# One decoder layer on one core: small rearrangements from the first projection to the MLP, and a merge whose weights are spread by matmuls alone

## The chip, the cores and the metric

The kernel runs on one core of one Trainium2 chip. The metric is the device time of one launch in microseconds (us), the median of several runs. Matmuls run on PE (TensorE), elementwise work on DVE (VectorE), ACT (ScalarE) and POOL (GpSimd), and SP (SyncE) issues the DMAs. Engines work side by side and meet at semaphores; each runs its own instructions in a fixed order.

## The reference, cut to what matters

A prompt group (2048 tokens) and a sample group (8 requests of 8 tokens with 2048 cached positions) pass through one layer, in float32:

```python
proj = rms_norm(x, ln1_g) @ w_in
q, k = head_rms(q, q_norm_g), head_rms(k, k_norm_g)        # 8 heads x 64
att = dilated_attention(q, k, v, ...)                      # 3 branches (128,1) (512,4) (2048,16),
                                                           # merged by their softmax denominators
r, k, v, xw, xa, xg = token_shifted(proj[..., 3 * A_W:])   # RWKV-7 columns
w_log = -softplus(-(w0 + tanh(xw) @ w_lora2)) - 0.5
a = sigmoid(a0 + xa @ a_lora2)
kk = kk / max(sqrt(sum(kk * kk, -1)), 1e-12)               # per head
y, S = wkv_scan(...)                                       # state update per token
bonus = sum(r * k * r_k, -1) * v                           # per head
mixed = concat([att, rw])
h = x + mixed @ w_out
y = h + square(relu(rms_norm(h, ln2_g) @ w_mlp1)) @ w_mlp2
```

The merge is `num / den` with `num = sum over branches of exp(mx - mall) * o`: each branch's output (64 dims per head) is multiplied by one weight per token and head.

## The kernel before, in words

The program is written as Python generators and handed to a scheduler that simulates the engines, fixes the order of each engine's instructions and adds the waits. Pieces marked urgent (the recurrence) go ahead of filler (the projection). Most products of two float32 operands are done as three matmuls of a rounded high part and a low remainder: `h` and `l` at the end of a name (`wh`/`wl`, `mh`/`ml`).

Times in the profiled execution:

1. **0 to about 1220 us, first stage.** The input projection (L332 for the recurrence's columns, L792 for q, k, v) is the filler. Between its matmuls runs the RWKV recurrence, in 9 units (8 of the prompt, 1 of the sample) of 4 head pairs `p`. `prep` of each unit and pair issues, among others: the two low-rank products (L394 with rows 0 to 63 of the tile `th`, L396 with rows 64 to 127), the sum of squares per head (L424, `sel2` as a 32-column stationary operand at column position `32 * p`), eight pairs of 64x64 products into `ps` (L433, L434), and the bonus sum (L438, a full 128x128 operand `blk1`).
2. **About 1220 to 1607 us, dilated attention** of four head pairs p = 0 to 3: scores (L1074, L1075), masks and maxima on DVE, exponentials on ACT, transposes (L1092), outputs (L1099). Tiles `pts` (4 buffers) take the transposed weights from PSUM. The merge of pair p (p = 0 to 2) runs as a side strand within the attention of pair p + 1; that of p = 3 has nothing beside it. A merge computes the normalised weights `scw` (3 branches x 128 per partition), splits them into a high and a low part `wh`, writes these to DRAM (`wD`, L1177) and reads them back as `wrow` (L1180) with 512 tokens in a row, and spreads them over the 64 dims of a head by 12 matmuls of 512 columns (L1187, stationary operand `wsel`); DVE multiplies each result into `ob` and adds the branches.
3. **1607 to 1904 us, output projection** (L1441) in 6 columns of 352 tokens, with the sample's attention between its matmuls: its cached keys and values come in 40 + 40 DMAs of 512 KB (`kv`, L1245 and L1278). Behind each column `square_sums` (L1409) forms the sums of squares that the second norm needs.
4. **1904 to 3359 us, MLP** in three token groups `g` of 2 x 352 tokens and eight rounds `r` each, by a Strassen-like scheme of seven products: `normed` (L1497 on PE, L1506 on DVE, `sums_b` L1476 to L1479 on POOL) prepares a group's operand, L1546 is the first product, L1592 the second. Weight tiles `wr` come by DMA (L1533, L1584), 8 buffers for the first. `reload` (L1486) fetches the next group's `h` (2.8 MB) back from DRAM.

All DMAs that the change touches are issued by SP, in one order.

Of the kernel before, what the change touches and what calls it, by code (L numbers as in the profile page):

```python
# [17 lines left out]
P = 128  # L18
# [19 lines left out]
def host_inputs(inp):  # L38
# [39 lines left out]
    out["sel2"] = f((ii[:, None] // 64) == np.arange(32)[None, :])  # L78
# [7 lines left out]
    sl = np.zeros((P, 4, P), np.float32)  # L86
    for ty in range(2):
        for g in range(4):
            for part in range(2):
                sl[part * 8 + g * 2 + ty, g, ty * 64:(ty + 1) * 64] = 1  # L90
# [10 lines left out]
    out["kc"] = f(keys(kc).reshape(8, 1280, 4, P).transpose(0, 2, 3, 1))  # L101
    out["vc"] = f(keys(vc).reshape(8, 10, P, 512))
# [69 lines left out]
def _build(ctx, tc, nc, I, O, dbg, upto):  # L172
# [73 lines left out]
    G.memset(tw, 0.0)  # L246

# [104 lines left out]
    def lora_prep(load):  # L352

        th = rw.tile([P, UT], F32, name="th")
        load(th)
        act(th[0:64], th[0:64], AF.Tanh)
        return th
# [29 lines left out]
    def prep(st, p, n, r, k, v, sample):  # L387
        nch = n // C
        L1, BK, GC, qS, qd, b1, vsc = (st[x] for x in ("L1", "BK", "GC", "qS", "qd", "b1", "vsc"))
        th = st["lora"]  # L390
# [3 lines left out]
        PE.matmul(zw[:, :n], lwa[0:64, ps_], th[0:64, :n], start=True, stop=True)  # L394
        za = ms()
        PE.matmul(za[:, :n], lwa[64:128, ps_], th[64:128, :n], start=True, stop=True)  # L396
# [63 lines left out]
    def bias_vectors():  # L460
# [17 lines left out]
        for h in range(8):  # L478
            nc.sync.dma_start(out=bvD[h:h + 1].rearrange("h p b n -> h p (b n)"), in_=bc(bv1[h:h + 1].rearrange("h b n -> h (b n)"), 1, P))
            yield  # L480
# [232 lines left out]
    def unit(g):  # L713
# [13 lines left out]
        st["lora"] = lora_prep(lambda t: nc.sync.dma_start(out=t, in_=xsD[12, :, us]))  # L727
# [22 lines left out]
    def sample_unit():  # L750
        st = new_unit()

        def padded(js, t):
            n = len(range(*js.indices(15)))
            c = rw3.tile([P, 3, NS], F32, name="xsc", bufs=1)[:, :n]
# [6 lines left out]
        st["lora"] = lora_prep(lambda t: padded(slice(12, 13), t.unsqueeze(1)))  # L762
# [351 lines left out]
    def merge(p, ob, st):  # L1114
# [60 lines left out]
        wD = dat.tile([6, 4, 8, P], F32, name="wD")  # L1175
        for g in range(4):
# [29 lines left out]
    wrow = at.tile([P, 3, 512], F32R, name="wrow")  # L1206
    G.memset(wrow.bitcast(F32), 0.0)
# [20 lines left out]
    def sample_attention(b, psa):  # L1228
# [12 lines left out]
        for k0, n, parts in runs:  # L1241
            ps = psa.tile([P, 512], F32, name="sc", tag="sp", bufs=2)
            for k1 in range(0, n, 256):
                kt = kv_tile().rearrange("p (q n) -> p q n", q=4)
                nc.sync.dma_start(out=kt, in_=I["kc"][b, :, :, k0 + k1:k0 + k1 + 256].rearrange("p q n -> q p n"))  # L1245
# [23 lines left out]
        for q0 in range(0, 11, 4):  # L1269
            bl = blocks[q0:q0 + 4]  # L1270
            vts = []
            for y in range(0, len(bl), 2):
                vt = kv_tile().rearrange("p (q n) -> p q n", q=2)
                kb = bl[y][2]
                if kb is None:
                    nc.sync.dma_start(out=vt[:8, 0], in_=vSD[b * 8:b * 8 + 8])
                else:
                    nc.sync.dma_start(out=vt, in_=I["vc"][b, kb:kb + 2].rearrange("k q f -> q k f"))  # L1278
# [137 lines left out]
    with pool(name="wo2", bufs=1) as wo2, pool(name="pwo", bufs=4, space=PSUM, side="right") as pwo, pool(name="psa", bufs=1, space=PSUM) as psa, pool(name="pst", bufs=1, space=PSUM) as pst:  # L1416
# [5 lines left out]
        for c0 in range(0, NT, NC_):  # L1422
# [9 lines left out]
            for k in order:  # L1432
                if (k, c0) not in mixed:
                    mixed[k, c0] = mix_panel(we if k >= 4 else wo2, k, c0)
            for o in range(KT):
                ps = pwo.tile([P, 512], F32, name="pwo")
                i = 0
                for k in order:
                    mh, ml = mixed[k, c0]
                    for a, b in ((woh, mh), (woh, ml), (wol, mh)):  # L1440
                        PE.matmul(ps[:, :NC_], a[k][:, o * P:(o + 1) * P], b, start=(i == 0), stop=(i == 3 * KT - 1))  # L1441
                        i += 1
# [5 lines left out]
            for i in range(NC_ // SQ):  # L1448
                square_sums(h, c0 // SQ + i, i * SQ, pst.tile([P, 512], F32, name="pst"), wo2)
# [7 lines left out]
    with pool(name="mm", bufs=1, side="right") as mm, pool(name="pm", bufs=8, space=PSUM) as pm:  # L1457
# [31 lines left out]
        def normed(g, h, mb):  # L1489
# [112 lines left out]
        for g in range(3):  # L1602
            late = []
            nh = reload(1) if g == 0 else None
            for r in range(8):
                hs = []
                for f in (2 * r, 2 * r + 1):
# [3 lines left out]
                    if g == 1 and r == 0:  # L1611
                        nh = nh or reload(2)
# [7 lines left out]
                second(r, hs, h, last, g * 2 * HT, beside)  # L1620
                for _ in beside:
# [38 lines left out]
```

## Time and profile before

| what | value |
|---|---|
| median of 3 timed runs | 3361.71 us (3357.81 to 3361.98) |
| profiled execution, own time | 3364.24 us |
| its span in the trace | 3362.5 us |
| PE busy | 3156.2 us, 94% |
| DVE, ACT, POOL busy | 2156.4, 1472.5, 982.1 us |
| DMA engines, mean | 124 GB/s over the span |

The profiled execution lies 1.74 us above its span and 2.53 us above the median of the timed runs. In the profile a busy PE is a pipelined one: the duration of a matmul is longer than the distance to the next, so costs of single matmuls are read as the distance from start to start. "PEclk" is the granted clock as a share of 2.4 GHz; the lower level, 1.2 GHz, reads 0.5.

### The profile page before, as it was taken

How to read it: one execution, taken by the hardware profiler on the slowest of the kernel's cores; microseconds unless marked ns; L12 is line 12 of the kernel's file. 1: busy time of each engine (PE TensorE's matmuls, PEld its weight loads, DVE VectorE, ACT ScalarE, POOL GpSimd, SP SyncE). 2: the span in 40 equal slices, each digit the busy share in tenths (PEclk: the TensorE clock that was granted, in tenths of full speed). 3: DMA queues.
4: the chain of work that ended last, by engine and by line, in shares of the span. 5: the costliest groups of instructions: out<-in, count | busy, mean ns of one | idle time of the engine just before them, and what ended most of it. 6: DMA issues, size and time to landing. Idle time of an engine off the chain costs nothing. (4 is left out here: it accounts for less than half of the span.)

```text
span 3362.5 us, 63750 instructions
## 1 busy us (share of the span) xinstructions
PE 3156.2 (94%) x24214; PEld 2847.8 (85%) x24214; DVE 2156.4 (64%) x4539; ACT 1472.5 (44%) x3497; POOL 982.1 (29%) x1146
## 2 busy tenths in 40 slices
PE   5999989999998979999899689999999999999999
PEld 5866876787787868888688579999899999899999
DVE  4655676677566435566544487676976767967675
ACT  4454665555545447677222233232432323433332
POOL 1003442354043100111000154343543434533332
PEclk9998999999998989999899789999999999999999
DMA  5465466456457393333767423222232222222222
GB/s 167 134 183 154 116 183 168 119 134 189 128 128 196 89 284 130 109 92 89 235 220 241 151 63 85 66 81 67 90 120 63 88 64 82 91 66 85 64 88 73
DMA packets 369495, 418.45 MB, mean 124 GB/s; under 512 B 117251, under 2 KB 230718, under 8 KB 369188
## 3 DMA queue, kind: packets, MB, share of 16 engines
q1 hardware_dynamic: 369188, 414.38, 41.5%
q8 instruction: 190, 3.11, 0.4%
q14 instruction: 117, 0.96, 0.1%
HBM read 325.52 MB, written 93.46 MB: 125 GB/s over the span
## 5 line engine op out<-in xcount | busy, mean ns | idle before, releaser
L185 ACT ACTIVATE wh<-wr 128x512 fp32r<-128x512 f32 x744 | 463.3, 625 | 812.5 <-PE pm L1592 473.7
L1592 PE MATMUL pm<-fh,wl 128*128 128x352 f32 x1536 | 495.7, 323 | 8.8 <-DVE wl L1466 8.8
L1592 PE MATMUL pm<-fh,wh 128*128 128x352 f32 x1536 | 493.4, 324 | 0.0
L1592 PE MATMUL pm<-fl,wh 128*128 128x352 f32 x1536 | 492.1, 323 | 0.3 <-DVE fl L182 0.3
L1546 PE MATMUL pm<-ml,wh 128*128 128x352 f32 x1344 | 436.6, 325 | 12.3 <-DVE ml L182 12.3
L1546 PE MATMUL pm<-mh,wh 128*128 128x352 f32 x1344 | 437.0, 326 | 11.3 <-ACT wh L185 8.4
L1546 PE MATMUL pm<-mh,wl 128*128 128x352 f32 x1344 | 434.1, 324 | 8.2 <-DVE wl L1466 8.1
L182 DVE TENSOR_TENSOR res<-pm,res 128x352 f32<-128x352 f32 x384 | 198.4, 522 | 287.8 <-PE pm L1592 285.0
L1466 DVE TENSOR_TENSOR wl<-wr,wh 128x512 fp32r<-128x512 f32 x432 | 362.0, 838 | 3.1 <-ACT wh L185 0.6
L1592 PEld LDWEIGHTS pm<-fh,wl 128*128 128x128 f32 x1536 | 289.9, 189 | 9.8 <-DVE wl L1466 9.8
L1592 PEld LDWEIGHTS pm<-fl,wh 128*128 128x128 f32 x1536 | 289.1, 189 | 0.8 <-DVE fl L182 0.6
L1592 PEld LDWEIGHTS pm<-fh,wh 128*128 128x128 f32 x1536 | 289.0, 189 | 0.6 <-ACT mh L185 0.2
L1546 PEld LDWEIGHTS pm<-ml,wh 128*128 128x128 f32 x1344 | 255.1, 190 | 18.3 <-DVE ml L182 18.0
L1546 PEld LDWEIGHTS pm<-mh,wh 128*128 128x128 f32 x1344 | 255.0, 190 | 13.5 <-ACT wh L185 10.1
L1546 PEld LDWEIGHTS pm<-mh,wl 128*128 128x128 f32 x1344 | 254.8, 190 | 11.2 <-DVE wl L1466 11.1
L182 DVE TENSOR_TENSOR wl<-wr,wh 128x512 fp32r<-128x512 f32 (+1 forms) x216 | 149.1, 692 | 156.8 <-ACT wh L185 149.5
L792 PE MATMUL pj<-wh,nh 128*128 128x256 f32 (+1 forms) x816 | 239.5, 294 | 6.3 <-ACT qks L185 5.0
L792 PE MATMUL pj<-wh,nl 128*128 128x256 f32 (+1 forms) x816 | 237.7, 292 | 4.6 <-DVE nl L182 4.6
L332 PE MATMUL pj<-nh,wh 128*128 128x512 f32 (+3 forms) x600 | 222.3, 374 | 16.3 <-ACT nh L185 9.9
L792 PE MATMUL pj<-wl,nh 128*128 128x256 f32 (+1 forms) x816 | 235.3, 289 | 0.0
L332 PE MATMUL pj<-nl,wh 128*128 128x512 f32 (+3 forms) x600 | 223.3, 373 | 4.6 <-DVE nl L182 4.5
L332 PE MATMUL pj<-nh,wl 128*128 128x512 f32 (+3 forms) x600 | 218.8, 366 | 0.3 <-DVE wl L182 0.3
(305 smaller groups left out, 7120.0 us busy)
## 6 DMA issues: line engine op xcount, KB each, us to landing
wr<-in_w SPq DMA_DIRECT2D x384, 256.0 KB
wr<-in_wr SPq DMA_DIRECT2D x120, 256.0 KB
wr<-in_wq SPq DMA_DIRECT2D x96, 256.0 KB
kv<-in_kc SPq DMA_DIRECT2D x40, 512.0 KB
kv<-in_vc SPq DMA_DIRECT2D x40, 512.0 KB
xsD<-xst SPq DMA_DIRECT2D x56, 256.0 KB
xrkv<-xsD SPq DMA_DIRECT2D x32, 384.0 KB
vt<-vD SPq DMA_DIRECT2D x48, 256.0 KB
```

The lines of the kernel that those rows point to most:

```text
L182: V.tensor_tensor(out, a, b, op)
L185: S.activation(out, in_, func, bias=bias, scale=scale, **kw)
L332: PE.matmul(ps[:m, :n], a[:, k, :m], b[h * 4 + k][:, c0:c0 + n], start=(h == 0 and i == 0), stop=(h == 1 and i == 11))
L792: PE.matmul(out, a[h * 2 + k][:, i * P:i * P + m], b[:, k, :], start=(h == 0 and q == 0 and i % 2 == 0), stop=(h == 3 and q == 5 and (i % ...
L1466: (G if pooled else V).tensor_tensor(wl, w, wh.bitcast(F32), ALU.subtract)
L1546: PE.matmul(ps, a[:, k], b[:, k], start=(n == 0), stop=(n == 11))
L1592: PE.matmul(ps, a[:, f], b[:, cs], start=(i == 0), stop=(i == 11))
```

## The change

First stage: `th` becomes two zero-padded halves, so that L394 and L396 contract over all 128 partitions; `sel2` becomes a slice of a wider table, so that L424 writes all 128 columns; L438 moves ahead of the `ps` products; the prompt's low-rank input comes in two DMAs of 64 partitions and the sample's through a tile and two POOL copies.

Attention: the merge reads `wh` directly as the moving operand. For each of the 12 results there are now 4 blocks of 128 columns times high and low part, 96 matmuls per pair instead of 12, and no `wD`, `wrow`. `wsel` is four times as large and comes in four DMAs through four `pts` buffers.

Sample attention: `kc` and `vc` lie in memory so that each partition's 4 KB are one piece. Output projection: in the first column, groups of four outputs take the recurrence's panels first.

MLP: `square_sums` of the last column moves behind round 0 of the first group; `reload` moves from round 0 to round 1; in group 0 `sums_b` runs on DVE for two of four blocks.

```diff
-    out["sel2"] = f((ii[:, None] // 64) == np.arange(32)[None, :])
+    out["sel2"] = f((ii[:, None] // 64) == np.arange(-96, 128)[None, :])
...
-    out["kc"] = f(keys(kc).reshape(8, 1280, 4, P).transpose(0, 2, 3, 1))
-    out["vc"] = f(keys(vc).reshape(8, 10, P, 512))
+    out["kc"] = f(keys(kc).reshape(8, 5, 256, 4, P).transpose(0, 1, 4, 3, 2))
+    out["vc"] = f(keys(vc).reshape(8, 5, 2, P, 512).transpose(0, 1, 3, 2, 4))
...
+    th = rw.tile([P, 2, UT], F32, name="th")
+    G.memset(th, 0.0)
...
-        PE.matmul(zw[:, :n], lwa[0:64, ps_], th[0:64, :n], start=True, stop=True)
+        PE.matmul(zw[:, :n], lwa[:, ps_], th[:, 0, :n], start=True, stop=True)
...
-        PE.matmul(za[:, :n], lwa[64:128, ps_], th[64:128, :n], start=True, stop=True)
+        PE.matmul(za[:, :n], lwa[:, ps_], th[:, 1, :n], start=True, stop=True)
...
-        PE.matmul(ssp[32 * p:32 * p + 32, :n], sel2, t2[:, :n], start=True, stop=True, tile_position=(0, 32 * p))
+        PE.matmul(ssp[:, :n], sel2[:, 96 - 32 * p:224 - 32 * p], t2[:, :n], start=True, stop=True)
...
+        bo = ms()
+        PE.matmul(bo[:, :n], blk1, t3[:, :n], start=True, stop=True)
+        tt(t3[:, :n], bo[:, :n], v, ALU.mult)
 
         ps = ms()
...
-        bo = ms()
-        PE.matmul(bo[:, :n], blk1, t3[:, :n], start=True, stop=True)
-        tt(t3[:, :n], bo[:, :n], v, ALU.mult)
...
-        wD = dat.tile([6, 4, 8, P], F32, name="wD")
-        for g in range(4):
-            nc.sync.dma_start(out=wD[:, g].rearrange("a r n -> r a n"), in_=wh[32 * g:32 * g + 8].rearrange("p x b n -> p (x b) n").bitcast(F32))
-        wr = wrow
-        for x in range(2):
-            nc.sync.dma_start(out=wr[x * 8:x * 8 + 8].bitcast(F32), in_=wD[3 * x:3 * x + 3].rearrange("b g (t c) n -> (g t) b (c n)", t=2))
-        yield
         yield
         for g in range(4):
             cs = slice(g * 512, (g + 1) * 512)
             for b in range(3):
                 ps = mp()
-                PE.matmul(ps, wsel[:, g], wr[:, b], start=True, stop=True)
+                for c in range(4):
+                    for x in range(2):
+                        PE.matmul(ps[:, c * P:(c + 1) * P], wsel[:, g, c], wh[:, x, b], start=(x == 0), stop=(x == 1))
...
-    wsel = at.tile([P, 4, P], F32R, name="wsel")
-    wsel0 = at.tile([P, 4, P], F32, name="wsel0", tag="pts", bufs=4)
-    nc.sync.dma_start(out=wsel0, in_=I["wsel"])
-    act(wsel, wsel0, AF.Copy)
...
+    wsel = at.tile([P, 4, 4, P], F32R, name="wsel")
+    for g in range(4):
+        wsel0 = at.tile([P, 4, P], F32, name="wsel0", tag="pts", bufs=4)
+        nc.sync.dma_start(out=wsel0, in_=I["wsel"][:, g])
+        act(wsel[:, g], wsel0, AF.Copy)
...
-            for i in range(NC_ // SQ):
-                square_sums(h, c0 // SQ + i, i * SQ, pst.tile([P, 512], F32, name="pst"), wo2)
+            if c0 + NC_ < NT:
+                for i in range(NC_ // SQ):
+                    square_sums(h, c0 // SQ + i, i * SQ, pst.tile([P, 512], F32, name="pst"), wo2)
...
-                sums_b(G, S, B11, B12, B21, B22)
+                sums_b(V if g == 0 and k % 2 else G, S, B11, B12, B21, B22)
...
-            nh = reload(1) if g == 0 else None
+            nh = None
...
-                    if g == 1 and r == 0:
-                        nh = nh or reload(2)
...
                 second(r, hs, h, last, g * 2 * HT, beside)
+                if g == 0 and r == 0:
+                    for i in range(20, 24):
+                        square_sums(res, i, (i - 16) * SQ, pm.tile([P, 512], F32, name="pm"), mw)
+                if g < 2 and r == 1:
+                    nh = reload(g + 1)
```

Three places in the order. On ACT, where the attention begins (the exponentials `e`, the first copies of transposed weights `pts`, the conversion of `wsel`), before:

```order
L185 ACTIVATE e,st<-e,st 128x256 x10
L185 ACTIVATE pts<-pt 128x384
L185 ACTIVATE e,st<-e,st 128x256
L185 ACTIVATE pts<-pt 128x512
L185 ACTIVATE e,st<-e,st 128x256 x2
L185 ACTIVATE ob_14818<-o 128x512
L185 ACTIVATE wsel<-wsel_14807 128x512
```

and after:

```order
L182 ACTIVATE e,st<-e,st 128x256 x10
L182 ACTIVATE wsel<-wsel_14811 128x512
L182 ACTIVATE wsel<-wsel_14814 128x512
L182 ACTIVATE pts<-pt 128x384
L182 ACTIVATE wsel<-wsel_14817 128x512
L182 ACTIVATE wsel<-wsel_14820 128x512
L182 ACTIVATE e,st<-e,st 128x256
L182 ACTIVATE pts<-pt 128x512
```

The conversions of `wsel` now stand ahead of the first two copies into `pts`. On PE, where the merge of pair 3 ends and the output projection (`pwo`) begins, before:

```order
L1099 MATMUL o<-pts,vt 64x128 x8
L1247 MATMUL sc<-kv,qbd 32x256 x8
L1187 MATMUL sc<-wrow,wsel 128x512 x12
L1441 MATMUL pwo<-mh,wo_19119 128x352
L1441 MATMUL pwo<-ml,wo_19119 128x352
```

and after:

```order
L1106 MATMUL o<-pts,vt 64x128 x7
L1247 MATMUL sc<-kv,qbd 32x256 x8
L1189 MATMUL sc<-wh_19483,wsel 128x128 x96
L1443 MATMUL pwo<-mh,wo_19361 128x352
L1443 MATMUL pwo<-ml,wo_19361 128x352
```

The place of the merge is the same, and no projection matmul goes ahead of it. On SP, between the sample's last loads (`kv`) and the MLP's weights (`wr`), before:

```order
L1276 DMA kv<-vSD 8x512
L1447 DMA hD<-res_21694 1024x1x352
L1486 DMA res_22477<-hD 128x8x704
L1533 DMA wr<-in_w 128x512 x8
L1584 DMA wr<-in_w 128x512 x8
```

and after:

```order
L1276 DMA kv<-vSD 8x512
L1543 DMA wr<-in_w 128x512 x2
L1456 DMA hD<-res_22013 1024x1x352
L1543 DMA wr<-in_w 128x512 x6
L1594 DMA wr<-in_w 128x512 x8
L1543 DMA wr<-in_w 128x512 x8
L1496 DMA res_24016<-hD 128x8x704
```

The reload `res<-hD` moved from ahead of the first weights to behind 24 of them.

## Rows read from the trace of the kernel before

**Rows 1.** Busy time by stage: window, length, then PE, PEld, DVE, ACT, POOL; granted clock, DMA share, GB/s.
```profile
200.00:1200.00 1000.00, 932.52 (x9014) 757.01 (x9013) 642.74 (x1284) 541.07 (x1237) 320.96 (x581) 0.95 0.56 151
1250.00:1600.00 350.00, 347.91 (x2808) 293.88 (x2806) 206.68 (x889) 249.80 (x868) 45.70 (x65) 0.99 0.36 113
1607.00:1633.00 26.00, 11.92 (x39) 6.85 (x32) 19.47 (x39) 4.60 (x10) 0.00 (x0) 0.56 0.40 136
1924.00:1968.00 44.00, 25.54 (x75) 18.68 (x76) 41.06 (x47) 13.15 (x29) 36.52 (x26) 0.58 0.10 32
1968.00:3359.00 1391.00, 1374.62 (x8575) 1368.73 (x8573) 984.06 (x1523) 471.29 (x867) 550.14 (x406) 1.00 0.26 80
```
**Rows 2.** Timeline of PE at one L394: start, duration, instruction.
```profile
341.16 0.28 PE L792 MATMUL pj<-wh,nh 128*128 128x256 f32 x1
341.37 0.70 PE L394 MATMUL ms<-th,lwa 64*128 64x256 f32 x2
...
342.22 0.28 PE L792 MATMUL pj<-wh,nl 128*128 128x256 f32 x1
342.34 0.28 PE L792 MATMUL pj<-wh,nh 128*128 128x256 f32 x1
```
**Rows 3.** The same at one L438, a full operand.
```profile
363.95 0.70 PE L438 MATMUL ms<-t,c_blk 128*128 128x256 f32 x2
...
364.60 0.28 PE L792 MATMUL pj<-wl,nh 128*128 128x256 f32 x1
```
**Rows 4.** Timeline of PE: a merge matmul in attention, and the next matmul.
```profile
1352.02 0.43 PE L1187 MATMUL ax<-wrow,wsel 128*128 128x512 f32 x1
1352.29 0.28 PE L1074 MATMUL sc<-kst,qst 128*128 128x128 f32 x1
```
**Rows 5.** Timeline of PE: 128-column matmuls of the first branch, then of a later one.
```profile
1219.89 0.22 PE L1074 MATMUL sc<-kst,qst 128*128 128x128 f32 x1
...
1220.29 0.33 PE L1074 MATMUL sc<-kst,qst 128*128 128x256 f32 x1
...
1591.77 0.39 PE L1075 MATMUL sc<-klo,qst 128*128 128x128 f32 x1
...
1592.42 0.39 PE L1074 MATMUL sc<-kst,qst 128*128 128x128 f32 x1
```
**Rows 6.** Timelines at the attention's start: SP, DVE, ACT.
```profile
1238.86 0.33 SPq L1203 DMA_DIRECT2D wsel<-in_wsel  x1
...
1231.41 0.55 DVE L995 COPY pts<-pt 128x384 f32<-128x384 f32 x1
...
1242.96 0.63 ACT L185 ACTIVATE wsel<-wsel 128x512 fp32r<-128x512 f32 x1 [2.47 <-DMA wsel<-in_wsel]
```
**Rows 7.** Timelines at the merge of pair 3: DVE, then PE.
```profile
1613.49 0.55 DVE L182 TENSOR_TENSOR wh<-scw,wh 128x384 fp32r<-128x384 f32 x1
...
1619.81 3.54 PE L1187 MATMUL sc<-wrow,wsel 128*128 128x512 f32 x6 [12.05 <-DMA wrow<-wD]
...
1629.75 0.66 PE L1441 MATMUL pwo<-mh,wo 128*128 128x352 f32 x1 [0.40 <-DVE ob L182]
```
**Rows 8.** PE's idle time ahead of matmuls on `kv`, by releaser: us in total, times.
```profile
  DMA kv<-in_kc: 6.6, 9
  DMA kv<-in_vc: 1.9, 2
```
**Rows 9.** Timelines at the MLP's start: PE, SP, ACT.
```profile
1906.48 0.32 PE L1409 MATMUL pst<-ones,sq 128*88 128x1 f32 x2 [2.36 <-DVE sq L182]
...
1914.71 2.68 PE L1497 MATMUL pm<-dg,ones 88*128 88x352 f32 x4 [1.14 <-DVE ssq L179]
1923.73 1.35 PE L1546 MATMUL pm<-mh,wh 128*128 128x352 f32 x2 [6.33 <-ACT wh L185]
...
1911.87 0.57 SPq L1486 DMA_DIRECT2D res<-hD  x1
...
1923.04 1.31 ACT L185 ACTIVATE wh<-wr 128x512 fp32r<-128x512 f32 x2 [1.70 <-DMA wr<-in_w]
```

More of the change, by code (lines that the diff above doesn't have):

```diff
@@ L85, in host_inputs @@
     out["oneh"] = _onehot()
-    sl = np.zeros((P, 4, P), np.float32)
-    for ty in range(2):
-        for g in range(4):
-            for part in range(2):
-                sl[part * 8 + g * 2 + ty, g, ty * 64:(ty + 1) * 64] = 1
+    kk, m = np.arange(P)[:, None, None, None], np.arange(P)
+    sl = f(kk == 32 * np.arange(4)[:, None, None] + np.arange(4)[:, None] + 4 * (m // 64))
     pp = np.arange(P)[:, None]
@@ L352, in lora_prep @@
     def lora_prep(load):
-        th = rw.tile([P, UT], F32, name="th")
         load(th)
-        act(th[0:64], th[0:64], AF.Tanh)
+        act(th[0:64, 0], th[0:64, 0], AF.Tanh)
         return th
@@ L389, in prep @@
         L1, BK, GC, qS, qd, b1, vsc = (st[x] for x in ("L1", "BK", "GC", "qS", "qd", "b1", "vsc"))
-        th = st["lora"]
         c3 = lambda ap: ap.rearrange("p (c t) -> p c t", t=C)
@@ L478, in bias_vectors @@
         for h in range(8):
-            nc.sync.dma_start(out=bvD[h:h + 1].rearrange("h p b n -> h p (b n)"), in_=bc(bv1[h:h + 1].rearrange("h b n -> h (b n)"), 1, P))
+            nc.sync.dma_start(out=bvD[h].rearrange("p b n -> p (b n)"), in_=bc(bv1[h].rearrange("b n -> (b n)"), 0, P))
             yield
@@ L726, in unit, with lora_in @@
         st["xgate"] = xgate
-        st["lora"] = lora_prep(lambda t: nc.sync.dma_start(out=t, in_=xsD[12, :, us]))
+        def lora_in(t):
+            for y in range(2):
+                nc.sync.dma_start(out=t[64 * y:64 * y + 64, y], in_=xsD[12, 64 * y:64 * y + 64, us])
+        lora_prep(lora_in)
         def inputs(p):
@@ L754, in padded @@
             n = len(range(*js.indices(15)))
-            c = rw3.tile([P, 3, NS], F32, name="xsc", bufs=1)[:, :n]
+            c = rw.tile([P, 3, NS], F32, name="xsc", tag="w", bufs=2)[:, :n]
             nc.sync.dma_start(out=c, in_=xsD[js, :, T:].rearrange("j q t -> q j t"))
@@ L760, in padded, with lora_in @@
             return t
-        st["lora"] = lora_prep(lambda t: padded(slice(12, 13), t.unsqueeze(1)))
+        def lora_in(t):
+            x = padded(slice(12, 13), rw3.tile([P, 3, UT], F32, name="xrkv")[:, 0:1])
+            for y in range(2):
+                G.tensor_copy(t[64 * y:64 * y + 64, y], x[64 * y:64 * y + 64, 0])
+        lora_prep(lora_in)
         def xgate():
@@ L1174, in merge @@
         tt(wh[:, 1], sc, wh[:, 0].bitcast(F32), ALU.subtract)
-        wD = dat.tile([6, 4, 8, P], F32, name="wD")
-        for g in range(4):
-            nc.sync.dma_start(out=wD[:, g].rearrange("a r n -> r a n"), in_=wh[32 * g:32 * g + 8].rearrange("p x b n -> p (x b) n").bitcast(F32))
-        wr = wrow
-        for x in range(2):
-            nc.sync.dma_start(out=wr[x * 8:x * 8 + 8].bitcast(F32), in_=wD[3 * x:3 * x + 3].rearrange("b g (t c) n -> (g t) b (c n)", t=2))
-        yield
         yield
@@ L1244, in sample_attention @@
                 kt = kv_tile().rearrange("p (q n) -> p q n", q=4)
-                nc.sync.dma_start(out=kt, in_=I["kc"][b, :, :, k0 + k1:k0 + k1 + 256].rearrange("p q n -> q p n"))
+                nc.sync.dma_start(out=kt, in_=I["kc"][b, (k0 + k1) // 256])
                 for p in range(4):
@@ L1277, in sample_attention @@
                 else:
-                    nc.sync.dma_start(out=vt, in_=I["vc"][b, kb:kb + 2].rearrange("k q f -> q k f"))
+                    nc.sync.dma_start(out=vt, in_=I["vc"][b, kb // 2])
                 vts.append(vt)
@@ L1434, in _build, with share @@
                     mixed[k, c0] = mix_panel(we if k >= 4 else wo2, k, c0)
-            for o in range(KT):
[L1436 to L1442, printed above, removed]
+            acc = {}
+            def share(o, ks):
+                ps = acc[o] if o in acc else pwo.tile([P, 512], F32, name="pwo")
+                acc[o] = ps
+                for k in ks:
+                    mh, ml = mixed[k, c0]
+                    for x, (a, b) in enumerate(((woh, mh), (woh, ml), (wol, mh))):
+                        PE.matmul(ps[:, :NC_], a[k][:, o * P:(o + 1) * P], b, start=(k == order[0] and x == 0), stop=(k == order[-1] and x == 2))
+                return ps
+            for o in range(KT):
+                if c0 == 0 and o % 4 == 0:
+                    for x in range(4):
+                        share(o + x, order[:4])
+                ps = share(o, order[4:] if c0 == 0 else order)
                 tt(h[:, o], ps[:, :NC_], h[:, o], ALU.add)
```

2 lines of the change are left out of this document (removed).

## The prediction

> **What bounds the kernel now.** I read the busy time by stage first, because the average (PE busy 94%) mixes stages with different limits. PE is the bound in three of them: 932.5 of 1000 us in the middle of the first stage, 347.9 of 350 in the attention, 1374.6 of 1391 in the steady MLP [rows 1]. Two short stretches are different. Between 1607 and 1633 us, where the last pair is merged, PE is busy 11.9 of 26 us and the granted clock is 0.56 on average, so between its two levels; between 1924 and 1968 PE has 25.5 of 44 and DVE 41.1, so DVE is the limit there, with POOL at 36.5 beside it [rows 1]. So in the first stage and in the attention the question for each edit is how much PE time it adds or takes; at the two seams it is which chain of waits ends last. Then I read the timeline of PE at single instructions, because modelled durations overlap: a cost is the distance from start to start.
>
> **Part by part.** All sums are made against the profiled execution, 3364.24 us with a span of 3362.5; the timed median, 3361.71, lies 2.53 us below, and the final time is given on that basis.
>
> *First stage.* At an L394 the projection's matmul before it starts at 341.16 and the second one behind it at 342.22 [rows 2]. Those 1.06 us hold two projection matmuls, which follow each other at 0.12 (342.22 to 342.34); so L394 costs 1.06 - 0.24 = 0.82 us. L438 has as many passes and columns but the full 128x128 operand: 363.95 to 364.60 with one projection matmul between is 0.65 - 0.12 = 0.53 [rows 3]. The difference, 0.29 us, is what the 64-row shape costs among 128-row neighbours, and the change makes that shape full. L394, L396 and L424 run once per unit and pair, 9 x 4 = 36 times each; L424 is another partial shape (32 columns), and I give all three the same 0.29: 108 x 0.29 = 31 us of PE at most. Some of it will not arrive: PE idles 67.5 of the 1000 us [rows 1], and where the recurrence's own chain is late a shorter matmul only lengthens an idle time; where a neighbour is a 64x64 product the shape changes anyway. I take two thirds, **-20**, bounds -31 and 0. Moving L438 ahead of the `ps` pairs removes nothing by itself that is not in this count. The extra DMA per unit and the two POOL copies of the sample are hidden: DMA share is 0.56 and POOL has 321 of 1000 us [rows 1]. The whole order of this stage is a new one, for which I leave 8 us on both sides.
>
> *Merge within the attention (pairs 0 to 2).* Today a spreading matmul of 512 columns takes 0.27 us up to the next start [rows 4]. It becomes 8 of 128 columns. For those there are two prices: 128-column matmuls in a row on the first branch, 1219.89 to 1220.29 for four, 0.10 to 0.11 each; on a later branch, whose keys are read at a stride, 1591.77 to 1592.42 for three, 0.22 each [rows 5]. `wh` and `wsel` are read contiguously, so I take the lower one: 8 x 0.11 = 0.88, so +0.61 per result, times 12 x 3 = 36: **+22**, and PE is busy 347.9 of 350 us there, so nearly all of it arrives; I enter +21. The upper bound is 36 x (8 x 0.22 - 0.27) = +54. The Trainium skill ("TensorE: Matmul & The Clock Gate", section "Back-to-back issue gap") gives about 81 ns for a sustained matmul of 128 columns; by it this term would be about 9 us smaller. That makes 3343, inside the forecast's own range below; the rows here say 0.10 to 0.11.
>
> *The load of `wsel`.* Today its DMA is issued at 1238.86 and the data are there at 1242.96, four microseconds later; the first copy into `pts` ran at 1231.41 [rows 6]. In the changed kernel the four raw tiles occupy all four `pts` buffers, and on ACT the conversions stand ahead of the first copy. So the first transposed weights cannot leave PSUM before about 1243 to 1246 instead of 1231. Queued behind it are the output matmuls, and by the PSUM buffers the next transposes; scores and exponentials go on. The loads of keys pace this stretch too, so a part is hidden: **+7**, bounds +3 and +13.
>
> *Merge of pair 3.* Its weights are split at 1614.04 (the operation at 1613.49 and 0.55), and PE starts spreading at 1619.81: the trip through DRAM is 5.8 of the 12.05 us of idle time [rows 7]. That goes. What is late next: PE starts at half clock with 8 matmuls per result, at twice 0.11 that is 1.8 us per result, where DVE needs about 0.8 (12 results between 1619.81 and 1629.75 [rows 7]). If the clock rises after some microseconds, the 12 results take about 13 us and the projection starts about 3 us earlier, with a warm clock besides; if it never does, 96 x 0.21 = 20 us from 1614.1, and it starts over 4 us later. **-4**, bounds -8 and +5. That the projection's first column takes the recurrence's panels first could have filled this wait, but on PE the 96 matmuls still stand in one block ahead of the first projection matmul: nothing.
>
> *Keys and values.* The new layout shortens at most PE's waits on these loads, 6.6 + 1.9 = 8.5 us on 11 occasions [rows 8]. Larger pieces might bring some of it: **-3**, bounds -8.5 and 0. The Trainium skill ("DMA: Bandwidth & Descriptors", section "Specifications") has full rate from 512 bytes on, and the pieces are 1 KB already; by it this term would be 0. No row here shows the same bytes in larger pieces.
>
> *MLP's start.* The last column's sums of squares stand alone on the path: idle time begins at 1904.1, and the first matmul of the norm comes at 1914.71 [rows 9]. The first group doesn't need those tokens. They move behind round 0, where DVE is busy 984 of 1391 us [rows 1] and hides some 20 operations. That gives 10 us, if the weights come as early. Today they are issued behind a reload of 2.8 MB, which goes out at 1911.87, and arrive at 1923.04, 1.70 us after ACT was ready [rows 9]; the reload now stands behind 24 of the weight loads, so the wait of 1.7 goes too, unless memory of the projection comes free late. **-11**, bounds -15 and -4. `sums_b` on DVE for two of four blocks is 8 operations: at the mean of POOL's instructions there 1.4 us each off POOL (36.52 / 26), at DVE's mean 0.87 each onto DVE (41.06 / 47) [rows 1]. DVE is the fuller one, but it is also who waits for POOL's sums: bounds -11 and +7, and I take 0.
>
> Sum: -20 + 21 + 7 - 4 - 3 - 11 + 0 = **-10 us**, so 3354 for an execution like the profiled one and 3352 on the basis of the median. Here 0.2%, about what a measurement of this kernel can tell from no change, is 6.7 us.
>
> **The rivals.** *First, the first stage gives nothing back:* the recurrence's chain, not PE, sets its pace, and the saved PE time turns into idle time. For it: 67.5 us of idle time and a clock below 1.00 [rows 1]. Against it: PE is 93% busy and the projection is there to fill. Net -10 + 20 = +10: 3372, slower. It decides from the point where less than about a tenth of the 31 us arrives (-10 + 20 - 3 is +7). *Second, the merge's 128-column matmuls cost what the strided ones do,* 0.22: +32 more, net +22: 3384. For it: most 128-column rows of the attention have that price. Against it: the contiguous four. The kernel turns slower by over 0.2% from 0.17 us per matmul on (16.7 / 288 above 0.11). *Third, all of PE's first-stage gain arrives and the load of `wsel` hides behind the loads of keys:* -11 and -4 more, net -25: 3337. *Fourth, the seams give nothing:* DVE's new operations eat the MLP's start and the cold merge the DRAM trip. Net -10 + 11 + 4 = +5: 3367, no difference.
>
> **How the numbers follow.** The forecast as summed 0.44 (its own range 3343 to 3360); the first rival 0.17; the second 0.08; the third 0.19; the fourth 0.12. Of the forecast's own 0.44 about 0.32 lies beyond 0.2%. With the third that is faster 0.51; the rest of the forecast and the fourth are same, 0.24; the first and second slower, 0.25. The range that leaves out 2 in 10 cuts the far ends of the second and third rivals: 3330 to 3379.
>
> **What would show it.** Right: the new L394, L396 and L424 at about 0.53 us from start to start, and the attention beginning some 20 us earlier than at 1219.89; the spreading matmuls at 0.11; first copies into `pts` some 12 us behind the first exponentials; the projection from about 13 us after the last split; the first L1546 about 9 us after the last projection matmul instead of 20. Wrong: an attention that begins at the old time, spreading matmuls of 0.2, or a first-stage order in which urgent work comes later than before, which would move the total by more than all single terms.

## The result: slower, and where the time went

| | median | runs | ratio to before, 95% interval |
|---|---|---|---|
| before | 3361.85 us | 6, 3354.67 to 3362.90 | |
| changed | 3388.47 us | 6, 3384.29 to 3397.47 | 1.0092 (1.0078 to 1.0106) |

The changed kernel is 0.9% slower, 27 us, where 10 us less were forecast; the time lies above the range's upper end, 3379. Its profiled execution took 3384.29 us (span 3382.5) against 3364.24 before, so the two traces differ by 20 us of the 27. To see where, both traces are cut at the same events: the first score matmul of the attention, its last output matmul, the first and the last matmul of the output projection, and the first L1592 (L1602 in the changed kernel) of rounds 0 and 1. The lengths, read from the starts of these instructions (the last one up to the end of the last matmul):

| stretch, us | before | changed | difference | forecast |
|---|---|---|---|---|
| first stage | 1219.9 | 1207.1 | -12.8 | -20 |
| attention (with the load of `wsel`) | 386.6 | 412.4 | +25.8 | +28 |
| last output matmul to projection (merge of pair 3) | 23.3 | 29.9 | +6.6 | -4 |
| output projection | 274.0 | 275.7 | +1.7 | -3 |
| projection's end to first L1592 of round 0 | 79.4 | 66.8 | -12.6 | -11 |
| from there to the first L1592 of round 1 | 57.3 | 67.9 | +10.6 | 0 |
| the rest of the MLP | 1318.2 | 1319.0 | +0.8 | 0 |

Three of these decide: the attention, the merge of pair 3, and the round that gives back what the MLP's start had gained. Busy time by stage in the changed kernel, columns as in [rows 1]:

```profile
200.00:1187.00 987.00, 904.43 (x8989) 763.35 (x8987) 644.85 (x1285) 538.20 (x1238) 320.33 (x580) 0.96 0.56 151
1250.00:1600.00 350.00, 349.26 (x2828) 299.02 (x2825) 199.61 (x830) 234.09 (x805) 43.93 (x62) 1.00 0.31 97
1632.00:1649.00 17.00, 17.00 (x82) 17.00 (x81) 11.44 (x17) 0.00 (x0) 0.00 (x0) 0.50 0.14 55
```

The last row is the surprise: in the last merge PE is busy all of 17 us and the granted clock is 0.50, its lower level of 1.2 GHz, throughout.

**The merge.** All picking matmuls by shape (count, duration min/median/max in ns), then the timeline of PE at the last merge, in the changed kernel:

```profile
L1189 PE MATMUL ax<-wh,wsel x288: 222/275/323, 1333.7 to 1580.2; 128*128 128x128 f32 x144
L1189 PE MATMUL sc<-wh,wsel x96: 414/415/477, 1628.7 to 1649.2; 128*128 128x128 f32 x96
```
```profile
1628.69 20.89 PE L1189 MATMUL sc<-wh,wsel 128*128 128x128 f32 x96 [7.96 <-ACT wh L182]
1649.37 0.60 PE L1443 MATMUL pwo<-mh,wo 128*128 128x352 f32 x1
```

Within the attention the distance from start to start is 0.112 us at the median, 11.2 us for each pair's 96, 33.5 us for the three. In the last merge it is 0.213 for all 96: 20.7 us from the first to the projection. In [rows 7] the same stretch was 9.9 us (1619.81 to 1629.75), behind 12.05 us of idle time. The DRAM trip did go (7.96 us idle instead of 12.05), and the matmuls then took 10.7 us more. The kernel before has the lower clock there too, though its 12 wide matmuls don't show it, because DVE is the limit beside them. Busy time by window, before:

```profile
1619.80:1629.80 10.00, 7.97 (x13) 3.45 (x13) 9.19 (x16) 0.00 (x0) 0.00 (x0) 0.50 0.14 54
```

**The MLP's start.** Timeline of PE in the changed kernel:

```profile
1926.93 1.42 PE L1507 MATMUL pm<-dg,ones 88*128 88x352 f32 x4 [1.50 <-DVE dg L179]
1931.03 0.66 PE L1556 MATMUL pm<-mh,wh 128*128 128x352 f32 x1 [2.68 <-ACT mh L182]
...
2026.21 0.32 PE L1409 MATMUL pm<-ones,sq 128*88 128x1 f32 x2 [3.24 <-DVE sq L179]
2028.33 0.45 PE L1409 MATMUL pm<-ones,sq 128*88 128x1 f32 x2 [1.81 <-DVE sq L179]
2030.59 0.45 PE L1409 MATMUL pm<-ones,sq 128*88 128x1 f32 x2 [1.80 <-DVE sq L179]
```

The norm's first matmul comes 1.5 us after the projection's end instead of 10.6 [rows 9], and the first L1556 5.6 us after it instead of 19.6. But the four sums of squares stand in a row in PE's order between round 0 and round 1, and PE waits for DVE's `sq` there much as it did at the old place: 3.24, 1.81 and 1.80 us, where it was 2.36, 1.80, 1.81 and 1.80. The row of sums lasts 8.2 us (2022.72 to 2030.90), and the product behind it starts at the lower clock:

```profile
2031.00:2035.00 4.00, 4.00 (x15) 4.00 (x15) 0.33 (x2) 0.43 (x1) 1.65 (x1) 0.50 0.87 333
```

Four microseconds at half clock are 2 us lost; with the 8.2 they are nearly all of the 10.6. The serial tail was moved, not hidden.

**The first stage** has the cheaper matmuls, but most of what they save is lost again. Timeline of PE at an L391, the former L394:

```profile
327.09 0.28 PE L799 MATMUL pj<-wh,nh 128*128 128x256 f32 x1
327.20 0.59 PE L391 MATMUL ms<-th,lwa 128*128 128x256 f32 x2
327.45 0.47 PE L799 MATMUL pj<-wl,nh 128*128 128x256 f32 x1
327.75 0.28 PE L799 MATMUL pj<-wh,nl 128*128 128x256 f32 x1
```

From 327.09 to 327.75 are 0.66 us where [rows 2] had 1.06, so 0.40 less in such a place. PE's busy time up to the attention falls from 1106 to 1080 us, 25.5 us; its idle time, counted from its first matmul, grows from 92 to 104. Part of the 25.5 is the clock: in these two executions 97 and 75 us of the busy time lie at the lower clock. With those counted half, an estimate from the 0.213 and 0.112 us of a picking matmul at the two levels, 1057 and 1043 us are left, 14 us less. Among PE's waits in the first stage of the changed kernel (total, times, longest) are two for a DMA round trip inside the recurrence:

```profile
PE yps L581 <- DMA tw<-xtd: 5.0, 3, 2.5
PE pu L581 <- DMA tw<-xtd: 2.5, 1, 2.5
```

Before, PE did not wait for this DMA at all.

**The load of `wsel`.** Timelines at the attention's start, ACT and then DVE:

```profile
1227.66 1.28 ACT L182 ACTIVATE wsel<-wsel 128x512 fp32r<-128x512 f32 x2 [9.74 <-DMA wsel<-in_wsel]
...
1228.32 0.56 DVE L1002 COPY pts<-pt 128x384 f32<-128x384 f32 x1 [11.04 <-ACT wsel L182]
```

ACT waits 9.74 us for the load, and DVE's first copy into `pts` 11.04 us for ACT: it comes 21.3 us after the first score matmul (1207.06), where it was 11.5 (1231.41 in [rows 6], after 1219.9).

### The profile page after: what moved, and what is told of

Same layout as the page of the kernel before. It is cut to its first block, busy times and chain, and to the rows that moved or that the text cites. A ratio compares the mean times of both kernels' runs of the same rounds, so it can differ in the third digit from the quotient of the medians.

```text
span 3382.5 us, 64409 instructions
## 1 busy us (share of the span) xinstructions
PE 3166.4 (94%) x24550; PEld 2902.5 (86%) x24550; DVE 2163.6 (64%) x4547; ACT 1474.7 (44%) x3500; POOL 972.9 (29%) x1140
## 4 chain that ended last, share of the span: by engine, by line
PE 73%; DVE 9%; DMA 9%; SPq 3%; issue 3%; POOL 3%; ACT 1%; DVEq 0%; POOLq 0%; ACTq 0%
PE pm L1602 20%; PE pm L1556 17%; PE pj L331 7%; PE pwo L1443 6%; PE pj L799 4%; PE o L1106 3%; PE pt L1099 3%; PE sc L1081 2%; PE sc L1082 2%; DVE ml L179 1%; DMA xg<-in_xg 1%; PE ax L1189 1%; DVE rl L1516 1%; DMA wr<-in_wq 1%; PE ax L1291 1%
## 5 line engine op out<-in xcount | busy, mean ns | idle before, releaser
L1602 PE MATMUL pm<-fh,wl 128*128 128x352 f32 x1536 | 496.1, 323 | 8.8 <-DVE wl L1476 8.8
L1602 PE MATMUL pm<-fh,wh 128*128 128x352 f32 x1536 | 493.5, 324 | 0.0
L1602 PE MATMUL pm<-fl,wh 128*128 128x352 f32 x1536 | 492.4, 323 | 0.5 <-DVE fl L179 0.5
L1556 PE MATMUL pm<-ml,wh 128*128 128x352 f32 x1344 | 437.3, 326 | 12.9 <-DVE ml L179 12.9
L1556 PE MATMUL pm<-mh,wh 128*128 128x352 f32 x1344 | 439.2, 328 | 10.3 <-ACT mh L182 10.3
L1556 PE MATMUL pm<-mh,wl 128*128 128x352 f32 x1344 | 436.5, 325 | 6.1 <-DVE wl L1476 4.8
L1602 PEld LDWEIGHTS pm<-fh,wl 128*128 128x128 f32 x1536 | 290.2, 189 | 9.8 <-DVE wl L1476 9.7
L1602 PEld LDWEIGHTS pm<-fl,wh 128*128 128x128 f32 x1536 | 289.5, 189 | 1.1 <-DVE fl L179 0.8
L1602 PEld LDWEIGHTS pm<-fh,wh 128*128 128x128 f32 x1536 | 289.3, 189 | 0.8 <-ACT mh L182 0.2
L1556 PEld LDWEIGHTS pm<-ml,wh 128*128 128x128 f32 x1344 | 256.6, 191 | 16.8 <-DVE ml L179 16.7
L1556 PEld LDWEIGHTS pm<-mh,wh 128*128 128x128 f32 x1344 | 256.5, 191 | 13.1 <-ACT mh L182 12.9
L1556 PEld LDWEIGHTS pm<-mh,wl 128*128 128x128 f32 x1344 | 256.2, 191 | 9.3 <-DVE wl L1476 7.5
L1480 POOL TENSOR_TENSOR wr<-wr 128x512 f32<-128x512 f32 x48 | 68.8, 1434 | 595.1 <-DVE wl L1476 502.8
L179 DVE TENSOR_TENSOR wl<-wr,wh 128x512 fp32r<-128x512 f32 (+1 forms) x216 | 150.3, 697 | 139.6 <-ACT wh L182 136.6
```

The costliest lines, as they stand in the source:

```text
L179: V.tensor_tensor(out, a, b, op)
L1480: G.tensor_tensor(S[0], A21, A22, ALU.add)
L1556: PE.matmul(ps, a[:, k], b[:, k], start=(n == 0), stop=(n == 11))
L1602: PE.matmul(ps, a[:, f], b[:, cs], start=(i == 0), stop=(i == 11))
```

## The experiments

Twelve kernels. All ratios are to runs of the kernel before on the same chip; its medians were 3360.42, 3357.13 and 3361.05 us in the three groups of four. The timed runs of one kernel lie up to 17 us apart, so where few microseconds matter the stage lengths of the traces are read beside the medians. The changed kernel ran in a group of its own: differences to it are differences of medians, and by the ratios they come out 1 to 3 us larger.

| kernel | what differs | median, us | ratio, 95% interval |
|---|---|---|---|
| a_oldmerge | changed, merge as before | 3357.82 | 0.9992 (0.9981 to 1.0004) |
| a_sqspread | changed, sums of squares spread | 3380.11 | 1.0061 (1.0044 to 1.0077) |
| a_warm | changed, 5 extra matmuls ahead of last merge | 3387.90 | 1.0086 (1.0070 to 1.0101) |
| b_stage1 | before, first stage's edits | 3358.87 | 1.0003 (0.9991 to 1.0014) |
| a_best | changed, old merge and spread sums | 3351.25 | 0.9978 (0.9966 to 0.9989) |
| a_warm8 | as a_warm, 8 extra matmuls | 3392.57 | 1.0106 (1.0087 to 1.0124) |
| b_newmerge | before, new merge | 3399.05 | 1.0121 (1.0108 to 1.0135) |
| b_mlp | before, MLP's start with spread sums | 3349.28 | 0.9973 (0.9961 to 0.9985) |
| b_mlp_sums | b_mlp and `sums_b` half on DVE | 3348.11 | 0.9961 (0.9946 to 0.9977) |
| a_mix | changed, wide matmuls in the last merge | 3396.97 | 1.0115 (1.0096 to 1.0133) |
| a_half | changed, half of the picking matmuls | 3369.40 | 1.0030 (1.0017 to 1.0042) |
| a_wsel | changed, own buffers for `wsel`'s loads | 3383.78 | 1.0074 (1.0059 to 1.0090) |

### Is it the merge? a_oldmerge, b_newmerge, a_half

a_oldmerge puts the lines with `wD`, `wrow` and the single `wsel` back into the changed kernel; b_newmerge puts the new lines alone into the kernel before. a_half leaves out the low part of the weights:

```diff
-                    for x in range(2):
-                        PE.matmul(ps[:, c * P:(c + 1) * P], wsel[:, g, c], wh[:, x, b], start=(x == 0), stop=(x == 1))
+                    for x in range(1):
+                        PE.matmul(ps[:, c * P:(c + 1) * P], wsel[:, g, c], wh[:, x, b], start=True, stop=True)
```

> The changed kernel with the merge, its wsel and the trip through DRAM as before. Theory (the 384 small matmuls are the loss): PE gets back 26 us in the attention, 3.5 at its start and 7 at the last merge, so 3388 - 36 = about 3352, below the kernel before. Rival (the loss is the new order of the first stage and of the queues, the merge is hidden): within 8 us of the changed kernel, 3380 or more.

> The kernel before with the new merge and its wsel alone. Theory (26 us in the three merges, 7 in the last, 4 to 6 at the load of wsel): 3360 + 37 = 3397. Rival (in the kernel before the merge has slack beside it that the changed first stage had used up): 3375 or less.

> The changed kernel with half of the picking matmuls: the low part of the weights is left out of the merge (4 instead of 8 matmuls per result). Theory (PE's time for them is the loss): 144 x 0.112 = 16 us less in the attention, the last merge down to DVE's 14 us from 20.7, 3388 - 22 = 3366. Rival (the loss is the load of wsel or the order, not the number): 3383 or more.

Measured: 31 us less than the changed kernel without the new merge, 42 us more than before with it alone, 19 us less with half of it. All three lie near their theories (3352, 3397, 3366) and far from the rivals. Merge and `wsel` are more than the whole loss. In b_newmerge the attention is 415.6 us long and the stretch of the last merge 30.4, against 386.6 and 23.3 before. In a_half the last merge is still at the lower clock, 48 matmuls in 10.9 us, but short enough that DVE is the limit behind it:

```profile
1627.13 10.89 PE L1189 MATMUL sc<-wh,wsel 128*128 128x128 f32 x48 [8.32 <-ACT wh L182]
1638.71 0.66 PE L1443 MATMUL pwo<-mh,wo 128*128 128x352 f32 x1 [0.68 <-DVE ob L179]
```

### Why is the last merge at the lower clock? a_warm, a_warm8, a_mix

a_warm (5) and a_warm8 (8) put float32 matmuls of 512 columns into PE's wait ahead of the last merge, with unused results; a_mix puts wide ones into the merge itself:

```diff
+        if p == 3:
+            ps = mp()
+            for i in range(8):
+                PE.matmul(ps, ident, sw[:, 2:6].rearrange("p a n -> p (a n)"), start=True, stop=True)
```
```diff
                 ps = mp()
+                if p == 3:
+                    for _ in range(1 if g or b else 4):
+                        PE.matmul(ps, wsel[:, 0, 0], wh.rearrange("p x b n -> p (x b n)")[:, 0:512], start=True, stop=True)
```

> The changed kernel with five more float32 matmuls of 512 columns, their results unused, in PE's wait ahead of the last merge. Theory (the 96 matmuls of the last merge run at the lower clock only because PE came from an idle stretch): granted clock 1.0 in the merge, 0.11 us per matmul, the merge then limited by DVE at about 13 us instead of 20.7, so 3388 - 8 = 3380. Rival (matmuls of 128 columns are slow by themselves there): the merge stays at 0.21 us per matmul, 3388 or a few us more.

> As the run with five extra matmuls, but with eight, so that PE's idle time ahead of the last merge shrinks from 3.7 us to about 1 and the clock is still at its upper level when the merge begins. Theory A (the idle stretch sets the clock): 0.11 us per matmul in the last merge, about 13 us for it by DVE, and 3380. Theory B (a row of 128-column matmuls doesn't hold the upper level, as the dips to 0.5 in the attention at a fully busy PE suggest): the merge begins at 0.11 and falls to 0.21 per matmul within it; total 15 to 20 us for the merge, 3383 to 3388.

> The changed kernel with 15 wide matmuls (512 columns, results overwritten) put into the last merge: four ahead of the first result and one ahead of each other. Theory (a row of 128-column matmuls alone doesn't raise the granted clock, wide ones among them do): the clock rises to 1.0 within the merge, 0.11 us per narrow matmul afterwards, merge about 16 us instead of 20.7, 3388 - 4 = 3384. Rival (nothing in that stretch raises it): 96 x 0.21 + 15 x 0.43, merge 27 us, 3394.

None of the three helped. In a_warm the idle stretch ahead of the merge was still 3.71 us, and the clock fell within it. In a_warm8 about 1 us of it was to be left; it was 2.65 us, so the run did not reach its own condition, and neither of its theories held: all 96 matmuls take 0.21 from the first on, and the median is 3392.57. In a_warm8, timeline of PE, then busy time by window (columns as in [rows 1]):

```profile
1630.67 7.13 PE L1163 MATMUL sc<-sw,ident 128*128 128x512 f32 x16
1640.45 20.89 PE L1194 MATMUL sc<-wh,wsel 128*128 128x128 f32 x96 [2.65 <-ACT wh L182]
1661.14 0.60 PE L1448 MATMUL pwo<-mh,wo 128*128 128x352 f32 x1
```
```profile
1638.00:1640.00 2.00, 0.00 (x0) 0.00 (x0) 1.29 (x2) 1.90 (x4) 0.00 (x0) 1.00 0.08 31
1640.00:1642.00 2.00, 1.55 (x7) 1.48 (x7) 1.18 (x3) 0.40 (x1) 0.00 (x0) 0.52 0.62 192
1642.00:1650.00 8.00, 8.00 (x39) 8.00 (x39) 4.53 (x7) 0.00 (x0) 0.00 (x0) 0.50 0.07 26
```

The clock is 1.00 up to 1640 and falls as the merge begins, behind 2.65 us without a matmul. So the price is the same whether the clock has just fallen or was low before, and the 8 extra matmuls only delayed the merge. Whether the idle stretch or the narrow matmuls made it fall, this run doesn't part: an idle stretch was left. A merge of pair 3 with no idle stretch ahead of it was not run. What the merge doesn't do is raise the clock again, although the profile shows no gap on PE for 20 us. In a_mix, with one wide matmul to eight narrow ones:

```profile
1640.78 1.80 PE L1192 MATMUL sc<-wh,wsel 128*128 128x128 f32 x8
1642.38 0.73 PE L1189 MATMUL sc<-wh,wsel 128*128 128x512 f32 x1
1642.91 1.80 PE L1192 MATMUL sc<-wh,wsel 128*128 128x128 f32 x8
```
```profile
1645.00:1665.00 20.00, 20.00 (x87) 19.08 (x85) 11.03 (x17) 0.00 (x0) 0.00 (x0) 0.50 0.10 40
```

the clock stays at 0.50 as well, for 27 us; my theory for this run fell and its rival's sum (27 us, 3394) held. In all of them the clock rises only within the projection's 352-column matmuls.

### The moved sums of squares: a_sqspread, b_mlp, b_mlp_sums

The squares of one of the four sums are issued ahead of the second product of each of rounds 0 to 3, and the one-column matmul behind it (`square_sums` becomes a generator with a `yield` ahead of its matmul):

```diff
+                sq = None
+                if g == 0 and r < 4:
+                    sq = square_sums(res, 20 + r, (4 + r) * SQ, None, mw, lambda: pm.tile([P, 512], F32, name="pm"))
+                    next(sq)
                 second(r, hs, h, last, g * 2 * HT, beside)
-                if g == 0 and r == 0:
-                    for i in range(20, 24):
-                        square_sums(res, i, (i - 16) * SQ, pm.tile([P, 512], F32, name="pm"), mw)
-                if g < 2 and r == 1:
+                for _ in sq or ():
+                    pass
+                if g < 2 and r == (1 if g else 4):
                     nh = reload(g + 1)
```

> The changed kernel, but the four late sums of squares are spread over rounds 0 to 3, their squares on ACT and DVE issued ahead of the second product and only the one-column matmul behind it. Theory (the four matmuls stand in a row in PE's order and wait for DVE, 10 us): that idle time goes, 3388 - 10 = 3378. Rival (DVE is full there and the idle time moves on to the next product): 3386 to 3390.

> The kernel before with the MLP's start alone: the last column's sums of squares spread over rounds 0 to 3 and the reloads later (sums_b stays on POOL). Theory (10 us of serial work leaves the path and nothing takes its place): first L1546 about 11 us after the last projection matmul instead of 20, 3360 - 10 = 3350. Rival (the start is bound by DVE and by the weights' arrival anyway): 3357 to 3362.

> The kernel before with the MLP's start (sums of squares spread over rounds 0 to 3, reloads later) and in addition sums_b on DVE for two of four blocks. Theory (POOL's sums are waited for there; the first L1592 comes 3 us earlier where DVE has two of them): 3349 - 3 = 3346, the lowest so far. Rival (DVE is the fuller engine, it costs what it saves): 3349 or more.

In b_mlp and in all kernels with spread sums the reload stands later as well, behind round 4 of the first group. All three came out near what the theory said: 8.4 us less than the changed kernel; 7.9 less than before; and with `sums_b` on DVE the lowest median of the study. In b_mlp the first L1546 came 5.6 us after the projection's end, not the 11 expected, but the first L1592 only 9.7 us earlier than before (69.7 us after the projection's last start instead of 79.4); part of the early start turns into waiting again. Timeline of PE in b_mlp at the end of round 0:

```profile
1995.49 0.32 PE L1596 MATMUL pm<-fh,wl 128*128 128x352 f32 x1
1995.65 0.24 PE L1411 MATMUL pm<-ones,sq 128*88 128x1 f32 x2
1995.75 0.41 PE L1550 MATMUL pm<-mh,wh 128*128 128x352 f32 x1
```

The sum is ready when PE comes to it, and the next product follows 0.1 us later. From the projection's end to the first L1592 of round 1 it takes 136.6 us before, 134.6 changed, 127.7 in b_mlp, 124.8 in b_mlp_sums; the last step, 2.9 us, is `sums_b` (between the two medians, from different groups, lie 1.2 us, with overlapping intervals, so for that step the trace is the evidence).

### The first stage: b_stage1, a_best

> The kernel before with the edits of the first stage alone (full-array low-rank products and sums of squares, L438 earlier, the low-rank input in two DMAs). Theory (PE's own time falls by 25 us and half of that turns into idle time): the attention begins 13 us earlier, 3362 - 13 = 3349. Rival one (all of PE's time arrives when nothing else is changed): 3337. Rival two (the recurrence sets the pace): 3360 to 3364.

> The changed kernel with both losses taken out: the merge and its wsel as before, and the late sums of squares spread over rounds 0 to 3. Theory (the two effects add): 3358 - 8 = 3350, 0.3% below the kernel before. Rival (the MLP's start and the spread squares share one limit, DVE): 3357, no difference.

b_stage1 is within 0.2% of the kernel before: theory and first rival fall in the total, and the second rival's number, no change, all but holds. The theory was right up to the attention: PE's busy time there is 1082 us instead of 1106, its idle time 105 instead of 92. The same holds for all: busy time averages 1104 us in the four profiles with the old first stage and 1083 in nine with the new one (without a_wsel), 21 us less; idle time 91 and 105, 14 us more. With the busy time at the lower clock counted half, the averages are 1058 and 1042: 16 us of work saved. Of the idle time, `tw<-xtd` has 0 to 0.8 us with the old first stage and 6.0 to 8.2 with the new one, so about half of the growth is the recurrence's own chain, as the second rival said. Whether the shorter matmuls or the new order laid that wait bare was not tried.

The attention begins at 1210.6. Over the profiles the first score matmul starts at 1214.3 to 1219.9 with the old first stage (before, b_newmerge, b_mlp, b_mlp_sums; mean 1217.3) and at 1207.1 to 1215.0 with the new one (nine profiles without a_wsel, in which the scores had moved; mean 1210.8): 6.5 us are gained. With the old merge they are lost in the attention:

| attention, old merge | length, us | of it at the lower clock, us |
|---|---|---|
| old first stage: before, b_mlp, b_mlp_sums | 386.6, 383.9, 388.0 | 10, 4, 7 |
| new first stage: b_stage1, a_oldmerge, a_best | 394.3, 394.1, 391.4 | 21, 24, 17 |

The right column sums twice the shortfall of the granted clock below 1.00 over windows of 5 us from 1250 to 1605. The profiled executions of b_stage1 and a_oldmerge are the slowest of their ten, so their rows lie at the upper end; a_best's is near its median. Such a stretch in b_stage1:

```profile
1302.00:1306.00 4.00, 4.00 (x26) 3.55 (x25) 1.34 (x7) 1.34 (x7) 0.00 (x0) 0.50 0.00 0
```

PE is busy without a gap, with 128-column score matmuls and transposes, and the clock is 0.50. Some 14 us more at half clock account for about 7 us where PE is the bound, which is the difference. It lies in one place, between the 201st and the 301st output matmul. Busy time by window of exactly that stretch, in the kernel before, in b_stage1 and in the changed kernel:

```profile
1295.46:1329.05 33.59, 33.59 (x314) 28.95 (x310) 16.21 (x89) 24.61 (x93) 2.19 (x6) 1.00 0.34 110
1286.03:1326.20 40.17, 40.17 (x316) 33.02 (x312) 17.44 (x96) 26.38 (x99) 2.50 (x7) 0.83 0.32 100
1286.38:1319.98 33.60, 33.60 (x314) 28.96 (x310) 16.21 (x89) 24.61 (x93) 2.19 (x6) 1.00 0.34 106
```

Nearly the same matmuls, in another order, take 6.6 us more, and a clock of 0.83 over 40.17 us is 6.8 us lost. The edits of the first stage also change the scheduler's order inside the attention; which of the changed places lets the clock fall was not tried and stays open. a_best, 3351.25, shows that the two repairs add (3350 was forecast), and by b_mlp beside it (3349.28) that with the old merge the first stage's edits bring nothing measurable in the end. With the new merge this dip is absent, and the attention lasts 412.4 to 419.8 us in the changed kernel, a_sqspread, a_warm, a_warm8 and a_mix (mean 416.3) and 415.6 in b_newmerge with the old first stage. So in the changed kernel the 6.5 us were kept, as far as single profiles can show it.

### The load of `wsel`: a_wsel

```diff
-        wsel0 = at.tile([P, 4, P], F32, name="wsel0", tag="pts", bufs=4)
+        wsel0 = at.tile([P, 4, P], F32, name="wsel0", bufs=2)
```

> The changed kernel with two raw buffers of their own for wsel's four loads instead of all four buffers of pts. Theory (the first copies into pts wait for these loads): the first outputs of the attention come as early as with the old wsel, 4 to 6 us less, 3388 - 5 = 3383. Rival (the loads of keys pace that stretch anyway): 3387 to 3390.

3383.78 is 4.7 us less than the changed kernel, the theory's number, but over runs that overlap (3380.47 to 3392.38 against 3384.29 to 3397.47), and the trace doesn't show the mechanism: the loads now go out ahead of the attention's keys, at 1211.33, the first score comes as late as 1226.7, and the first copy into `pts` at 1232.33; the 65th output matmul starts at 1251.2, later than the 1245.4 of the changed kernel. Inconclusive. The price of the place is read from the stage instead: from the first score matmul to the 65th output matmul, which lies ahead of the first merge, it takes 33.0 us before and 38.4 in the changed kernel, 5.4 more. In b_newmerge, where the first stage is the old one, it takes 40.7, 7.7 more, with DVE's first copy into `pts` waiting 11.98 us for ACT's `wsel`.

## Why the prediction was wrong, point by point

The sum missed by 37 us: 13 in the first stage, 11 in the merge of pair 3, 9 at the MLP's start, 3 at the keys and values, 1 in the attention.

**First stage, -20.** Two steps failed. The price was too high: 0.29 us for each of 108 places gave 31, but the saving is 16 us of work (21 us of busy time on average, some of it the clock); the 0.40 of the one clean place is not the mean of the 108, and L424 got its price without a row of its own. And "I take two thirds" failed: idle time grew by 14 us, and 6.5 of the 21 arrived at the attention. That is in large part the first rival's mechanism, the recurrence's chain, and half of it is a DMA wait that the prediction had no term for. Its number, 3372, is not tested by the total, because the other terms moved too. What arrived was kept in the changed kernel; with the old merge the attention gave it back, by the clock.

**Merge within the attention, +21, and `wsel`, +7.** Both held: the 36 results take 33.5 us of PE's starts instead of 11.6, +22, and the load of `wsel` costs 5.4 to 7.7; together +25.8 in the two profiles of the result and +29 in b_newmerge, against +28. In part two small errors cancel: the old matmul takes 0.32 us on average and not the 0.27 of the one place read, the new eight 0.93 and not 0.88. The second rival (0.22) did not occur at these three pairs. The 81 ns that the prediction quotes from the Trainium skill ("TensorE: Matmul & The Clock Gate", section "Back-to-back issue gap") appear in no row here; 0.112 us does. (By 81 ns the term would have been 8 us smaller, 0.029 x 288, not 9.)

**Merge of pair 3, -4.** Here the working held both ends, a clock that rises after some microseconds and one that "never does", and took the wrong one: "96 x 0.21 = 20 us" is what happened, 20.7 measured. The step that failed is the assumption that the clock would rise once PE was busy. The trip through DRAM gave 4.1 us and not 5.8, and with the 10.7 the stretch is 6.6 us longer, beyond the bound of +5. A row of the kernel before spoke against the rise: through its own last merge, 10 us long, the clock was 0.50. The second rival's price, 0.22, thus came true at this one place, by the clock and not by a stride.

**Keys and values, -3.** Nothing that the profiles show: the projection takes 270.2 to 275.7 us over all of them with either layout, 274.0 before, and PE's waits for these loads are 7.5 us in the changed kernel and 11.2 in a_best against 8.5. The term of 0, by the Trainium skill ("DMA: Bandwidth & Descriptors", section "Specifications"), was the nearer one.

**MLP's start, -11.** The size was near up to the first L1592 (-12.6), but in part by luck: -9.7 are the moved sums and the weights (b_mlp), and -3 are `sums_b`, which the sum had at 0. What failed is "hides some 20 operations": it asked only whether DVE has room, and not where the four matmuls stand in PE's order. They stood in a row, with the same wait for DVE ahead of all but the first as at the old place [rows 9]; the order on PE would have told it. Round 0 to round 1 gave back 10.6, so -2 is left of -11.

The sum of terms, corrected: -7 + 22 + 7 + 7 + 0 - 2 = +27, with the first stage's gain averaged over the profiles and `wsel` as in b_newmerge. The medians differ by 27 too, but the two profiles by 20, and each term is uncertain by some microseconds, so the exact agreement is luck.

## What to carry to other kernels

Moving serial work off a path helps only if each engine that takes part in it finds its operand ready at the new place: look at where the moved instructions stand on the in-order engine that waits, not at the room on the engine that computes. Replacing a DMA round trip by more matmuls is dear where PE is the bound (22 us for 36 results). Behind an idle stretch, price a chain of narrow matmuls at the lower clock for its whole length as well, as one end of the range; here it was that end in every profile. A shorter matmul helps only where PE does not wait anyway: compare the idle time, not only the busy time, and compare busy times at the same clock. A gain at the end of one stage is booked only when the next stage keeps it.

## What the hardware showed

A PE that the profile shows busy without a gap did not always have the upper clock: 96 matmuls of 128 columns ran 20.7 us at 0.50 behind 8 us (changed kernel), 3.7 us (a_warm) and 2.65 us (a_warm8) of idle time, and a mix with 512-column ones 27 us, while blocks of eight within the attention ran at 1.00 and 0.112 us each. And the clock fell to 0.50 in the attention at a fully busy PE as well (b_stage1, 1302 to 1306), in all 0 (changed kernel) to 24 us (a_oldmerge) between 1250 and 1605: 40.2 us for a stretch that took 33.6 at 1.00 with nearly the same matmuls in another order. What in the order decides, no run shows.
